# Linear attention: a head's recurrence emitted in eight steps instead of one piece

## The chip, the cores and the metric

The kernel runs on one core of a Trainium2 chip. The core has five engines that the kernel uses: TensorE (PE in the profile; its weight loads are listed apart as PEld), VectorE (DVE), ScalarE (ACT), GpSimd (POOL) and SyncE (SP), whose queue issues the DMA transfers. Each engine works through its own list of instructions in order. The metric is the device time of one execution, in microseconds; the median of the runs is given.

## The reference

The program is one inference step of a network of four layers over 640 tokens (512 latent tokens and 128 context tokens) of 1024 channels. Each layer has another token mixer: HGRN2 (a gated linear recurrence), a gated convolution, an RG-LRU recurrence and latent attention. Each ends in a layer norm. The change touches the first layer, whose mixer is this:

```python
def hgrn2_mixer(h, w_in, lb, norm_g, w_out, s0):
    q, f_fw, f_bw, i, g = jnp.split(h @ w_in, ...)
    q = (jax.nn.silu(q) * HG_KDIM ** -0.5).reshape(b_, n, HG_HEADS, HG_KDIM)
    v = i.reshape(b_, n, HG_HEADS, HG_VDIM)
    for d, fl in enumerate((f_fw, f_bw)):
        f = (lb[d] + (1 - lb[d]) * jax.nn.sigmoid(fl)).reshape(b_, n, HG_HEADS, HG_KDIM)
        args = (q, 1 - f, v, jnp.log(f))        # flipped in time for d == 1
        o, s = gla_chunk(*args, s0[:, d])
    o = rms_norm(outs[0] + outs[1], norm_g.reshape(HG_HEADS, HG_VDIM))
    y = (o.reshape(b_, n, HG_V) * jax.nn.silu(g)) @ w_out
```

There are 8 heads with 128 key and 128 value channels. The function gla_chunk is the recurrence S <- f * S + k v^T, o = q S, taken in chunks: scores inside a chunk (q times decay against k over decay, masked to the causal part), and a state that is carried from chunk to chunk. The states after the last token are outputs too.

## The kernel before, in words

Activations lie with channels on the 128 partitions and the 640 tokens along the row. A product with fp32 accuracy is made of three matmuls on a high part and a low part of both factors. ACT casts the high part of a weight block (wh, L80) and DVE subtracts it from the block for the low part (wl, L82); the cast is marked so that it keeps the place that it has in the program text. `next_w` is called at the start of each product; it returns that product's block and prepares the block that is wanted some products later.

A Python function with a list scheduler behind it writes the program: each operation gets its place in its engine's list in the order of the text, except where the scheduler moves a ready one ahead. In layer 0 (`hgrn`) the loop over `HG_ORDER` goes through the heads ("h") and the gates ("g"). For a head there are two forget products (psmm, 48 matmuls of 128x320: 8 blocks of the inner dimension, three split products, two halves of the tokens), whose tanh is th0 and th1, then the query product (psmm; psmh for head 0) and, for even heads, the value product of two heads (pv: five token tiles of 24 matmuls of 128x256; the first 12 of a tile use one weight block, the other 12 the next). A gate has one product. Small matmuls of the adaLN vectors (psA) are put between.

The function `gla` is the recurrence of one head. Its parts, with the names that the trace shows: f and k from th (ACT, L744, L746); prefix and suffix decays pre and suf as scans (DVE, L748 to L754); inv, the inverse decay, by Ln (ACT, L761, L762) and Exp (ACT, L873), which need two sets of function tables; block decays B, S and kr, ku (DVE); the transposes of ku (pst, PE, L798) and their copy kt (ACT, L800); state updates (psu, PE, L804) and the states s (DVE, L836); scores attS and attP (PE, L849 to L863); outputs po and pp (PE, L885, L887); the RMS norm, with squares on ACT (L893), the mean and the power on POOL (L894, L895) and the scaling on DVE (on, L897); transposes back (pm, pn, PE, L905) and the copies into o (ACT, L906, L907).

Before, `gla(h)` is written in one piece: a hook in `mtile` calls it at the fourth block of the product that follows the head's query and value products. So all casts that the value product wants are already in the text. The last part (pm, pn and the copies) is kept back and written after the second product that follows.

Of the kernel before, what the change touches and what calls it, by code (L numbers as in the profile page):

```python
# [9 lines left out]
F32 = mybir.dt.float32  # L10
F32R = mybir.dt.float32r
U32 = mybir.dt.uint32
AF = mybir.ActivationFunctionType
# [3 lines left out]
P = 128  # L17
D = 1024
KT = D // P
TS_ = 512  # L20
TP = 128
T = TS_ + TP
HALF = T // 2
SPL = (slice(0, 384), slice(384, T))
NT = T // P
# [25 lines left out]
class Kernel:  # L51
# [127 lines left out]
    def mtile(self, nk=KT, xh=None, xl=None, halves=False):  # L179

        nc = self.nc
        xh = self.xh if xh is None else xh
        xl = self.xl if xl is None else xl
        wh, wl = self.next_w()
        if halves:
            ps = [self.psg.tile([P, 512], F32, name="psmh", tag="g") for _ in range(2)]
            out = [p[:, :HALF] for p in ps]
        else:
            ps = self.psmm.tile([P, 2, 512], F32, name="psmm", tag="mm")
            out = ps = ps[:, :, :HALF]  # L190
            ps = [ps[:, hf, :] for hf in range(2)]
        for k in range(nk):
            if self.hook and k == 3:
                hook, self.hook = self.hook, None
                hook()
            for w, x, first, last in ((wh, xh, True, False), (wh, xl, False, False), (wl, xh, False, True)):
                for hf in range(2):
                    nc.tensor.matmul(ps[hf][:, :HALF], lhsT=w[:, k, :], rhs=x[:, k, hf * HALF:(hf + 1) * HALF],  # L198
                                     start=(first and k == 0), stop=(last and k == nk - 1))
        return out  # L200
# [46 lines left out]
    def token_sums(self, pool):  # L247
# [17 lines left out]
        self.split(*t[4], b21)  # L265
        self.tops = t

    def mpair(self):

        nc = self.nc  # L270
        ws = [self.next_w() for _ in range(2)]
        pss = []
        for c in SPL:
            ps = self.psmm.tile([P, 2, 512], F32, name="psmm", tag="mm")
            ps = ps[:, :, :c.stop - c.start]
            for n, (wh, wl) in enumerate(ws):
                hook = None
                if self.pend and n == 1:
                    hook, self.pend = (HOOK, self.pend), None
                self.mm3(ps[:, n, :], [(wh[:, k, :], wl[:, k, :], self.xh[:, k, c], self.xl[:, k, c])  # L280
                                       for k in range(KT)], hook)
            pss.append(ps)
        return pss

# [262 lines left out]
    def start(self):  # L547

        nc, tc = self.nc, self.tc
        with ExitStack() as ctx:  # L550
# [59 lines left out]
            for q in range(4):  # L610
# [4 lines left out]
                        part(q, u)  # L615
                finish(q)

    HG_ORDER = (("h", 0), ("h", 1), ("h", 2), ("g", 0), ("h", 3), ("g", 1), ("h", 4), ("g", 2), ("h", 5), ("g", 3),
                ("h", 6), ("g", 4), ("h", 7), ("g", 5), ("g", 6), ("g", 7))

    def hgrn(self):
        nc, tc, I = self.nc, self.tc, self.I
        with ExitStack() as ctx:
            gc = ctx.enter_context(tc.tile_pool(name="gc", bufs=1))
            g1 = ctx.enter_context(tc.tile_pool(name="g1", bufs=1))
            g2 = ctx.enter_context(tc.tile_pool(name="g2", bufs=2))
# [38 lines left out]
            hng = gc.tile([P, HEADS], F32, name="hng")  # L665
# [1 line left out]
            zb = gc.tile([P, 256], mybir.dt.bfloat16, name="zb")  # L667
            nc.gpsimd.memset(zb, 0.0)
            self.hc = (c0, c1, nc1, hng, m16, mtri, mb, attm, ln64, zb)
            vt, wait = None, 0  # L670
            tails = []
            for kind, h in self.HG_ORDER:
                if (kind, h) == ("g", 6):
                    self.pend = tails.pop()
                    pss = self.mpair()
                    for hf in range(2):
                        for n in range(2):
                            hh = 6 + n
                            sg = self.silu2h(g1, pss[hf][:, n], "silut")
                            oc = self.o[:, hh, SPL[hf]]  # L680
                            nc.vector.tensor_tensor(out=oc, in0=oc, in1=sg, op=ALU.mult)
                    break
                if kind == "g":
                    ps = self.mtile()
                    wait += 1
                    sg = self.silu2h(g1, ps, "silut")
                    nc.vector.tensor_tensor(out=self.hv(self.o[:, h, :]), in0=self.hv(self.o[:, h, :]), in1=sg, op=ALU.mult)
                    continue
                th = []
                for d in range(2):  # L690
                    ps = self.mtile()
                    wait += 1
                    if tails and wait >= 2:
                        tails.pop()()
                    t = g2.tile([P, T], F32, name=f"th{d}", tag=f"th{d}", bufs=1)
                    nc.scalar.activation(out=self.hv(t), in_=ps, func=AF.Tanh, scale=0.5)
                    th.append(t)
                ps = self.mtile(halves=h == 0)
                qt = g1.tile([P, T], F32, name="qt", tag="silut")
                q = g2.tile([P, T], F32, name="q", tag="q")  # L700
                qs = 0.5 * P ** -0.5
                if h == 0:
                    parts = [(self.hv(qt)[:, n], self.hv(q)[:, n], ps[n]) for n in range(2)]
# [7 lines left out]
                if h % 2 == 0:  # L711
                    vt = g2.tile([P, NT, 256], F32, name="vt", tag="vt")
                    ws = [self.next_w() for _ in range(2)]
                    for i0 in range(0, NT, 2):
                        pv = self.psmm.tile([P, 2, 512], F32, name="pv", tag="mm")
                        n = min(2, NT - i0)
                        for i in range(n):
                            tok = slice((i0 + i) * P, (i0 + i + 1) * P)
                            self.mm3(pv[:, i, 0:256], [(self.xh[:, k, tok], self.xl[:, k, tok], ws[k // 4][0][:, k % 4, :],
                                                        ws[k // 4][1][:, k % 4, :]) for k in range(KT)])  # L720
                        nc.scalar.copy(out=vt[:, i0:i0 + n, :], in_=pv[:, 0:n, 0:256])  # L721
                wait = 0
                vh = vt[:, :, (h % 2) * P:(h % 2) * P + P]
                self.hook = lambda h=h, th=th, q=q, vh=vh: tails.append(self.gla(h, th, q, vh, g1, g2, gd))

    def gla(self, h, th, q, vt, g1, g2, gd):
        nc, I = self.nc, self.I
        c0, c1, nc1, hng, m16, mtri, mb, attm, ln64, zb = self.hc
        NB = T // 16

        def b3(ap, a, b):
            return ap.rearrange("p (a b) -> p a b", a=a, b=b)
        qint, states = [], []
        psP = self.psg.tile([P, 2, P], F32, name="attP", tag="g")

        def half(ap, w):
            return ap.rearrange("p (n w b) -> p n w b", w=2, b=16)[:, :, w, :]
# [27 lines left out]
        def direction(d, k, p, r, inv):  # L765
# [17 lines left out]
            if d == 1:  # L783
# [8 lines left out]
            ku = g1.tile([P, T], F32, name="ku", tag="ku")  # L792
            nc.vector.tensor_tensor(out=b3(ku, NB, 16), in0=b3(kr, NB, 16), in1=S[2].unsqueeze(2).to_broadcast([P, NB, 16]),
                                    op=ALU.mult)
            tiles = (0, 1, 2, 4) if d == 0 else (1, 2, 3, 4)
            pst = self.psg.tile([P, 4, P], F32, name="pst", tag="g")
            for n, i in enumerate(tiles):
# [1 line left out]
            kt = g1.tile([P, 4, P], F32, name="kt", tag="kt", bufs=2)  # L799
            nc.scalar.copy(out=kt, in_=pst)  # L800
            yield
            psu = self.psg.tile([P, 4, P], F32, name="psu", tag="g")
            for n, i in enumerate(tiles):
                nc.tensor.matmul(psu[:, n, :], lhsT=kt[:, n, :], rhs=vt[:, i, :], start=True, stop=True)  # L804
            qp = gd.tile([P, T], F32, name="qp", tag="qp")
            nc.vector.tensor_tensor(out=qp, in0=q, in1=p, op=ALU.mult)
            qrel, krel = inv, k
# [9 lines left out]
            for src, scl, n, g, w, nm in ((kr, S[1], 5, 4, er, "kh"), (qp, B[1], 5, 4, la, "qh"),  # L817
# [8 lines left out]
            nc.vector.tensor_tensor(out=b3(qi, 32, 16), in0=b3(qp[:, :TS_], 32, 16),  # L826
                                    in1=B[2][:, :32].unsqueeze(2).to_broadcast([P, 32, 16]), op=ALU.mult)
            qint.append(qi)

            s0 = g2.tile([P, P], F32, name=f"s0{d}", tag=f"s0{d}")  # L830
            nc.sync.dma_start(out=s0, in_=I["state_hgrn"][d, h])
# [8 lines left out]
            fin = g2.tile([P, P], F32, name="fin", tag="fin")  # L840
            nc.scalar.copy(out=fin, in_=psu[:, 3, :])
            nc.sync.dma_start(out=self.O["new_state_hgrn"][d, h], in_=fin)

            psS = self.psg.tile([P, 4, P], F32, name="attS", tag="g")
            pss = [psS[:, i, :] if i < 4 else psP[:, d, :] for i in range(NT)]
            for i, ps in enumerate(pss):
# [24 lines left out]
        inv = [invert(d, *dec[d]) for d in range(2)]  # L871
        for d in range(2):
            nc.scalar.activation(out=inv[d], in_=inv[d], func=AF.Exp, scale=-1.0, bias=ln64[:, 0:1])  # L873
        stages = [direction(d, *dec[d], inv[d]) for d in range(2)]
        for st in stages:
            for _ in st:
                pass
        att = gd.tile([P, T], F32, name="att", tag="suf")
        nc.vector.tensor_tensor(out=att, in0=attm[0], in1=attm[1], op=ALU.add)
        po = self.psg.tile([P, 4, P], F32, name="po", tag="g")  # L880
# [17 lines left out]
                                op=ALU.mult)  # L898
        nc.vector.tensor_scalar(out=on[:, TS_:], in0=pp, scalar1=r5[:, 4:5], scalar2=None, op0=ALU.mult)

        def tail():
            pm = self.psg.tile([P, TS_], F32, name="pm", tag="g")
            pn = self.psg.tile([P, P], F32, name="pn", tag="g")
            for i in range(NT):
                nc.tensor.transpose(pm[:, i * P:(i + 1) * P] if i < 4 else pn, on[:, i * P:(i + 1) * P], self.ident)  # L905
            nc.scalar.activation(out=self.o[:, h, :TS_], in_=pm, func=AF.Copy, scale=hng[:, h:h + 1])  # L906
            nc.scalar.activation(out=self.o[:, h, TS_:], in_=pn, func=AF.Copy, scale=hng[:, h:h + 1])  # L907
        return tail


    def taps(self, y, x, offs, wv):
# [610 lines left out]
    def build(self):  # L1522
# [7 lines left out]
        self.weights(wlist)  # L1530
        self.credit, self.rate = -2.0, 0.0
        self.sw = None
        self.pend = self.hook = None
        self.adaq, self.adafin = [], []
        self.start()
        for l in range(self.NL):
# [158 lines left out]
```

## Time and profile before

| what | value |
|---|---|
| median of 3 runs | 1456.24 us (1455.66 to 1457.84) |
| profiled execution, its time | 1453.07 us |
| its span on the core | 1451.3 us |
| mean granted TensorE clock | 0.995 |
| PE busy | 1401.8 us, 97% of the span |
| DVE busy | 1085.7 us, 75% |
| ACT busy | 751.2 us, 52% |

The span is what the profiler saw from the first to the last instruction. The granted clock is the share of full speed (2.4 GHz) that the throttle gave. Layer 0's products and recurrences lie at about 45 to 440 us of the span.

### The profile page before, as it was taken

The numbers are of one execution on the slowest core, as the hardware profiler recorded it, in microseconds if no ns is written. First come the engines' busy times: TensorE is split into PE (matmuls) and PEld (weight loads), VectorE is DVE, ScalarE is ACT, GpSimd is POOL, SyncE is SP. The second block draws the span as 40 slices with busy tenths as digits, with TensorE's granted clock in tenths as the row PEclk, the third lists the DMA queues.
The fourth block names the chain that finished last, engine by engine and source line by source line (L and its number), as shares of the span: only waits on it lengthen the run. The fifth ranks groups of instructions, "written<-read, shape, count | busy, mean of one in ns | idle before, by whom it ended". The sixth has DMA issues, their size and how long they took to land.

```text
span 1451.3 us, 26592 instructions
## 1 busy us (share of the span) xinstructions
PE 1401.8 (97%) x10762; PEld 1283.0 (88%) x10762; DVE 1085.7 (75%) x1987; ACT 751.2 (52%) x1350; POOL 88.0 (6%) x195
## 2 busy tenths in 40 slices
PE   6999999999999999999999999999999999999997
PEld 4898989989989899999998989899999888888795
DVE  4778587477668778878786999786656868677777
ACT  2657366356543644544426677632642466566630
POOL 0000000000000100000000011100110200000002
PEclk9999999999999999999999999999999999999999
DMA  9322334233246324443452434442213100000041
GB/s 347 121 90 85 100 116 136 82 110 114 85 142 211 139 77 158 146 145 117 143 192 88 146 131 144 139 152 84 67 62 128 57 27 10 25 30 30 30 146 72
DMA packets 51369, 160.50 MB, mean 111 GB/s; under 512 B 5984, under 2 KB 13488, under 8 KB 49456
## 3 DMA queue, kind: packets, MB, share of 16 engines
q1 hardware_dynamic: 51248, 158.82, 32.3%
q8 instruction: 84, 1.38, 0.4%
q14 instruction: 37, 0.30, 0.1%
HBM read 149.69 MB, written 9.10 MB: 109 GB/s over the span
## 4 chain that ended last, share of the span: by engine, by line
PE 70%; DVE 13%; ACT 10%; DMA 4%; issue 3%; POOL 1%; SPq 0%; POOLq 0%; DVEq 0%; ACTq 0%
PE psmm L198 13%; PE psx L217 7%; PE pso L176 4%; PE pso L177 4%; PE pso L175 4%; PE psz L217 3%; PE poa L1447 3%; PE psmm L1078 2%; DVE wl L82 2%; PE ptp L1434 2%; PE psy L217 2%; PE psA L353 2%; DVE tr L1108 1%; PE psmm L176 1%; PE psS L175 1%
## 5 line engine op out<-in xcount | busy, mean ns | idle before, releaser
L198 PE MATMUL psmm<-xh,wh 128*128 128x320 f32 x784 | 183.9, 316 | 2.6 <-ACT vt L721 2.1
L198 PE MATMUL psmm<-xh,wl 128*128 128x320 f32 x784 | 182.8, 312 | 0.0
L198 PE MATMUL psmm<-xl,wh 128*128 128x320 f32 x784 | 180.5, 311 | 0.0
L80 ACT CAST wh<-wraw 128x1024 fp32r<-128x1024 f32 (+4 forms) x129 | 127.2, 998 | 97.9 <-PE pso L177 42.7
L82 DVE TENSOR_TENSOR wl<-wraw,wh 128x1024 fp32r<-128x1024 f32 (+4 forms) x129 | 148.2, 1159 | 27.6 <-ACT wh L80 27.2
L176 PE MATMUL pso<-wl,xh 128*128 128x256 f32 (+1 forms) x464 | 148.7, 321 | 1.5 <-DVE wl L82 1.5
L175 PE MATMUL pso<-wh,xh 128*128 128x256 f32 (+1 forms) x464 | 149.3, 323 | 0.1
L177 PE MATMUL pso<-wh,xl 128*128 128x256 f32 (+1 forms) x464 | 148.5, 320 | 0.0
L198 PEld LDWEIGHTS psmm<-xh,wh 128*128 128x128 f32 x784 | 129.6, 188 | 11.5 <-issue 3.9
L198 PEld LDWEIGHTS psmm<-xh,wl 128*128 128x128 f32 x784 | 131.5, 188 | 1.0 <-issue 0.6
L198 PEld LDWEIGHTS psmm<-xl,wh 128*128 128x128 f32 x784 | 131.1, 188 | 1.4 <-issue 1.2
L176 PEld LDWEIGHTS pso<-wl,xh 128*128 128x128 f32 x464 | 87.4, 188 | 8.7 <-DVE wl L82 2.1
L175 PEld LDWEIGHTS pso<-wh,xh 128*128 128x128 f32 x464 | 87.2, 188 | 7.4 <-ACT xh L163 0.4
L177 PEld LDWEIGHTS pso<-wh,xl 128*128 128x128 f32 x464 | 87.3, 188 | 7.2
L1418 ACT ACTIVATE pe<-psS,mx 128x768 f32<-128x768 f32 (+1 forms) x80 | 63.7, 797 | 38.8 <-DVE mx L1416 38.4
L1416 DVE TENSOR_REDUCE mx<-psS 128x1 f32<-128x768 f32 (+1 forms) x80 | 65.3, 817 | 7.8 <-PE psS L177 7.1
L1434 PE MATMUL ptp<-ident,pe 128*128 128x128 f32 x400 | 56.8, 273 | 0.8 <-ACT pe L1418 0.8
L176 PE MATMUL psmm<-xl,wh 128*128 128x384 f32 (+1 forms) x160 | 49.8, 311 | 0.3 <-DVE xl L166 0.3
L175 PE MATMUL psmm<-xh,wh 128*128 128x384 f32 (+1 forms) x160 | 49.9, 312 | 0.0
L1447 PE MATMUL poa<-pT,v 128*64 128x256 f32 (+1 forms) x416 | 48.8, 377 | 0.7 <-ACT pT L1436 0.4
L177 PE MATMUL psmm<-xh,wl 128*128 128x384 f32 (+1 forms) x160 | 49.2, 308 | 0.0
L1434 PEld LDWEIGHTS ptp<-ident,pe 128*128 128x128 f32 x400 | 46.4, 140 | 2.4 <-ACT pe L1418 1.1
(501 smaller groups left out, 3756.5 us busy)
## 6 DMA issues: line engine op xcount, KB each, us to landing
wraw<-in_wpack SPq DMA_DIRECT2D x109, 512.0 KB
araw<-in_ada_rest SPq DMA_DIRECT2D x80, 512.0 KB
praw<-in_wpack SPq DMA_DIRECT2D x14, 1024.0 KB
araw<-in_ada_first SPq DMA_DIRECT2D x16, 512.0 KB
zdram<-z SPq DMA_DIRECT2D x10, 512.0 KB
gateb<-gate_dram SPq DMA_DIRECT2D x6, 512.0 KB
z<-zdram SPq DMA_DIRECT2D x6, 512.0 KB
wraw<-in_wpack SPq DMA_DIRECT2D x8, 320.0 KB
```

Of the source, the lines that this page charges most:

```text
L80: self.tc.keep_in_program_order(nc.scalar.copy(out=wh[:, :n], in_=raw[:, :n]))
L82: nc.vector.tensor_tensor(out=wl[:, :n], in0=raw[:, :n], in1=wh[:, :n].bitcast(F32), op=ALU.subtract)
L175: nc.tensor.matmul(ps, lhsT=ah, rhs=bh, start=(i == 0), stop=False)
L176: nc.tensor.matmul(ps, lhsT=ah, rhs=bl, start=False, stop=False)
L177: nc.tensor.matmul(ps, lhsT=al, rhs=bh, start=False, stop=(i == n - 1))
L198: nc.tensor.matmul(ps[hf][:, :HALF], lhsT=w[:, k, :], rhs=x[:, k, hf * HALF:(hf + 1) * HALF], start=(first and k == 0), stop=(last and k = ...
L217: nc.tensor.matmul(ps, lhsT=u[:, k, :], rhs=v[:, k, :], start=(first and st and k == 0), stop=(en and k == 3), skip_group_check=True)
L353: nc.tensor.matmul(ps[32 * j:32 * j + 32, :], lhsT=self.csil[:, k, :], rhs=raw[:, j * 256:(j + 1) * 256], start=(k == 2 * u), stop=(k == 2 ...
L1416: nc.vector.reduce_max(out=mx, in_=ps[:, :nk], axis=AX.X, negate=True)
L1418: nc.scalar.activation(out=pe[:, :nk], in_=ps[:, :nk], func=AF.Exp, bias=mx[:, 0:1], accum_out=g["sm"][:, n, hp:hp + 1])
L1434: nc.tensor.transpose(pt[:, kk, :], pe[:, (k0 + kk) * P:(k0 + kk + 1) * P], self.ident)
L1447: nc.tensor.matmul(po[hp * 64:(hp + 1) * 64, 0, :nq], lhsT=v4[:, kt, vc + hp * 64:vc + (hp + 1) * 64], rhs=g["pt"][hp][:, kk, :nq], start= ...
```

## The change

`gla` becomes a generator of eight steps. `hgrn` makes the generator of a head as soon as both th tiles exist, before the query product, and takes the first step at once: decays of both directions, all Ln and Exp, and the block decays, kr and ku of direction 0. The other steps have due times in estimated microseconds; `tick` adds an estimate for each block of a product (0.88), each value tile (2.8) and each half of a pair of gates, and takes every step that is due. The steps go through the two directions in turn (transposes and kt; score operands; psu and states; scores), then come the output and the norm, and last pm and pn with the copies. What is left of a head is taken before the next head's generator begins and, for the last step, after the head's gate product. The order of the heads and gates changes, psu moves behind the score operands, and the tile attP is taken when the first scores are written. The diff, cut:

```diff
...
         for k in range(nk):
-            if self.hook and k == 3:
-                hook, self.hook = self.hook, None
-                hook()
+            self.tick(0.88)
             for w, x, first, last in ((wh, xh, True, False), (wh, xl, False, False), (wl, xh, False, True)):
...
+    def tick(self, us):
...
+        self.now += us
+        for g in list(self.gens):
+            while g in self.gens and g[1] <= self.now:
+                self.step(g)
...
+    def step(self, g):
+        g[3] += 1
+        try:
+            g[1] = g[2] + next(g[0])
+        except StopIteration:
+            self.gens.remove(g)
...
                                        for k in range(KT)], hook)
+                self.tick(24 * (c.stop - c.start) / 2200)
             pss.append(ps)
...
-    HG_ORDER = (("h", 0), ("h", 1), ("h", 2), ("g", 0), ("h", 3), ("g", 1), ("h", 4), ("g", 2), ("h", 5), ("g", 3),
-                ("h", 6), ("g", 4), ("h", 7), ("g", 5), ("g", 6), ("g", 7))
+    HG_ORDER = (("h", 0), ("h", 1), ("g", 0), ("h", 2), ("h", 3), ("g", 1), ("g", 2), ("h", 4), ("h", 5), ("g", 3),
+                ("h", 6), ("h", 7), ("g", 4), ("g", 5), ("g", 6), ("g", 7))
...
             self.hc = (c0, c1, nc1, hng, m16, mtri, mb, attm, ln64, zb)
-            vt, wait = None, 0
-            tails = []
+            vt = None
+            done = {}
...
+            def finish(h, tail=True):
...
+                g = done[h]
+                while g in self.gens and (tail or g[3] < 8):
+                    self.step(g)
             for kind, h in self.HG_ORDER:
                 if (kind, h) == ("g", 6):
-                    self.pend = tails.pop()
                     pss = self.mpair()
+                    finish(7)
                     for hf in range(2):
...
                     ps = self.mtile()
-                    wait += 1
+                    finish(h)
                     sg = self.silu2h(g1, ps, "silut")
...
                     ps = self.mtile()
-                    wait += 1
-                    if tails and wait >= 2:
-                        tails.pop()()
                     t = g2.tile([P, T], F32, name=f"th{d}", tag=f"th{d}", bufs=1)
...
                     th.append(t)
+                if h:
+                    finish(h - 1, False)
+                qv = {}
+                g = [self.gla(h, th, qv, g1, g2, gd), 0.0, self.now, 0]
+                done[h] = g
+                self.gens.append(g)
+                self.step(g)
                 ps = self.mtile(halves=h == 0)
                 qt = g1.tile([P, T], F32, name="qt", tag="silut")
-                q = g2.tile([P, T], F32, name="q", tag="q")
+                q = qv["q"] = g2.tile([P, T], F32, name="q", tag="q")
                 qs = 0.5 * P ** -0.5
...
                                                         ws[k // 4][1][:, k % 4, :]) for k in range(KT)])
+                            self.tick(2.8)
                         nc.scalar.copy(out=vt[:, i0:i0 + n, :], in_=pv[:, 0:n, 0:256])
-                wait = 0
-                vh = vt[:, :, (h % 2) * P:(h % 2) * P + P]
-                self.hook = lambda h=h, th=th, q=q, vh=vh: tails.append(self.gla(h, th, q, vh, g1, g2, gd))
...
-    def gla(self, h, th, q, vt, g1, g2, gd):
+                qv["vt"] = vt[:, :, (h % 2) * P:(h % 2) * P + P]
...
+    def gla(self, h, th, qv, g1, g2, gd):
...
             return ap.rearrange("p (a b) -> p a b", a=a, b=b)
-        qint, states = [], []
-        psP = self.psg.tile([P, 2, P], F32, name="attP", tag="g")
+        qint, states, both = [], [], []
...
+        due = (10, 11, 22.5, 24, 26, 29, 32, 35) if h % 2 == 0 else (8, 9, 12, 15, 18, 21.5, 25, 29)
...
                                     op=ALU.mult)
+            yield
             tiles = (0, 1, 2, 4) if d == 0 else (1, 2, 3, 4)
...
             yield
-            psu = self.psg.tile([P, 4, P], F32, name="psu", tag="g")
-            for n, i in enumerate(tiles):
-                nc.tensor.matmul(psu[:, n, :], lhsT=kt[:, n, :], rhs=vt[:, i, :], start=True, stop=True)
+            q = qv["q"]
             qp = gd.tile([P, T], F32, name="qp", tag="qp")
...
             qint.append(qi)
+            yield
+            vt = qv["vt"]
+            psu = self.psg.tile([P, 4, P], F32, name="psu", tag="g")
+            for n, i in enumerate(tiles):
+                nc.tensor.matmul(psu[:, n, :], lhsT=kt[:, n, :], rhs=vt[:, i, :], start=True, stop=True)
...
+            yield
...
+            if d == 0:
+                both.append(self.psg.tile([P, 2, P], F32, name="attP", tag="g"))
+            psP = both[0]
             psS = self.psg.tile([P, 4, P], F32, name="attS", tag="g")
...
             nc.scalar.activation(out=inv[d], in_=inv[d], func=AF.Exp, scale=-1.0, bias=ln64[:, 0:1])
-        stages = [direction(d, *dec[d], inv[d]) for d in range(2)]
-        for st in stages:
-            for _ in st:
-                pass
+        da, db = [direction(d, *dec[d], inv[d]) for d in range(2)]
...
+        for ds, t in zip(((da,), (da, db), (da,), (da, db), (da, db), (db,), (db,)), due):
+            for st in ds:
+                next(st, None)
+            yield t
+        vt = qv["vt"]
         att = gd.tile([P, T], F32, name="att", tag="suf")
...
-        def tail():
-            pm = self.psg.tile([P, TS_], F32, name="pm", tag="g")
-            pn = self.psg.tile([P, P], F32, name="pn", tag="g")
-            for i in range(NT):
-                nc.tensor.transpose(pm[:, i * P:(i + 1) * P] if i < 4 else pn, on[:, i * P:(i + 1) * P], self.ident)
-            nc.scalar.activation(out=self.o[:, h, :TS_], in_=pm, func=AF.Copy, scale=hng[:, h:h + 1])
-            nc.scalar.activation(out=self.o[:, h, TS_:], in_=pn, func=AF.Copy, scale=hng[:, h:h + 1])
-        return tail
+        yield due[7]
+        pm = self.psg.tile([P, TS_], F32, name="pm", tag="g")
+        pn = self.psg.tile([P, P], F32, name="pn", tag="g")
+        for i in range(NT):
+            nc.tensor.transpose(pm[:, i * P:(i + 1) * P] if i < 4 else pn, on[:, i * P:(i + 1) * P], self.ident)
+        nc.scalar.activation(out=self.o[:, h, :TS_], in_=pm, func=AF.Copy, scale=hng[:, h:h + 1])
+        nc.scalar.activation(out=self.o[:, h, TS_:], in_=pn, func=AF.Copy, scale=hng[:, h:h + 1])
...
         self.sw = None
-        self.pend = self.hook = None
+        self.pend = None
+        self.gens, self.now = [], 0.0
         self.adaq, self.adafin = [], []
```

In the rows that follow, the number behind a name tells tiles of the same name apart. ACT, head 0, from the second forget product's tanh (th1) on. wh4 is the second weight block of the value product, qt the query's tanh. Before:

```order
L696 ACTIVATE th1_575<-psmm_526 128x640
L80 CAST wh4_578<-wraw4_577 128x1024
L744 ACTIVATE f_805<-th0_518,lbc0_461,lbc1_459 128x640
L707 ACTIVATE qt_633<-psmh_583 128x320
L707 ACTIVATE qt_633<-psmh_584 128x320
L80 CAST wh5_642<-wraw5_641 128x1024
```

Changed, from the first Ln of head 0 on (the tanh, f and k stand ahead of it):

```order
L785 ACT_TABLE_LOAD
L785 ACTIVATE inv_599<-suf_585 128x20x16
L786 ACTIVATE inv_599<-pre_583 128x20x16
L785 ACTIVATE inv_602<-pre_594 128x20x16
L905 ACT_TABLE_LOAD
L905 ACTIVATE inv_599<-inv_599,ln64_443 128x640
L786 ACT_TABLE_LOAD
L786 ACTIVATE inv_602<-suf_596 128x20x16
L730 ACT_TABLE_LOAD
L730 ACTIVATE qt_684<-psmh_634 128x320
L905 ACTIVATE inv_602<-inv_602,ln64_443 128x640
L80 CAST wh4_629<-wraw4_628 128x1024
```

The cast of wh4 stood right behind th1 and ahead of the first f; now it stands behind all Ln and Exp of both directions and four table loads.

PE, the value product of head 0, at the passage from its first weight block (wh3, wl3) to its second (wh4, wl4). Before, in the first token tile:

```order
L175 MATMUL pv_653<-wh3_521,xh_102 128x256
L176 MATMUL pv_653<-wl3_522,xh_102 128x256
L177 MATMUL pv_653<-wh3_521,xl_103 128x256
L175 MATMUL pv_653<-wh4_578,xh_102 128x256
L176 MATMUL pv_653<-wl4_579,xh_102 128x256
L177 MATMUL pv_653<-wh4_578,xl_103 128x256
```

Changed (pv_704 is the first token tile pair's first, pv_798 the next bank; the rows begin with the last matmuls that use the first weight block):

```order
L175 MATMUL pv_798<-wh3_521,xh_102 128x256
L176 MATMUL pv_798<-wl3_522,xh_102 128x256
L177 MATMUL pv_798<-wh3_521,xl_103 128x256
L823 MATMUL pst_753<-ident_74,ku_626 128x128 x4
L175 MATMUL pv_704<-wh4_629,xh_102 128x256
L175 MATMUL pv_798<-wh4_629,xh_102 128x256
L176 MATMUL pv_704<-wl4_630,xh_102 128x256
L177 MATMUL pv_704<-wh4_629,xl_103 128x256
```

Before, 12 matmuls with the first block were followed by those with the second. Now 24 with the first block stand ahead, of two banks, then the four transposes, then all that need wh4.

ACT, head 2, from the second forget product on. Before, wh12 is the second weight block of head 2's value product; f, k and inv are head 2's own:

```order
L696 ACTIVATE th1_1601<-psmm_1543 128x640
L906 ACTIVATE o_104<-pm_1592,hng_465 128x512
L907 ACTIVATE o_104<-pn_1593,hng_465 128x128
L80 CAST wh12_1604<-wraw12_1603 128x1024
L744 ACTIVATE f_1875<-th1_1601,lbc0_461,lbc1_459 128x640
L746 ACTIVATE k_1879<-th1_1601,lbc1_459,lbnc1_463 128x640
L762 ACT_TABLE_LOAD
L762 ACTIVATE inv_1886<-pre_1870 128x20x16
L761 ACTIVATE inv_1889<-pre_1881 128x20x16
L873 ACT_TABLE_LOAD
L873 ACTIVATE inv_1886<-inv_1886,ln64_443 128x640
```

Changed, where wh13 is the second weight block of head 2's value product; the rows are head 2's too, and pm_1725 belongs to head 1:

```order
L770 ACTIVATE k_1668<-th1_1651,lbc1_459,lbnc1_463 128x640
L905 ACT_TABLE_LOAD
L905 ACTIVATE inv_1675<-inv_1675,ln64_443 128x640
L785 ACT_TABLE_LOAD
L785 ACTIVATE inv_1678<-pre_1670 128x20x16
L942 ACTIVATE o_104<-pm_1725,hng_465 128x512
L943 ACTIVATE o_104<-pn_1726,hng_465 128x128
L832 COPY k_1668<-kr_1895 128x20x16
L786 ACTIVATE inv_1678<-suf_1672 128x20x16
L905 ACT_TABLE_LOAD
L905 ACTIVATE inv_1678<-inv_1678,ln64_443 128x640
L80 CAST wh13_1719<-wraw13_1718 128x1024
```

Before, wh12 stood right behind th1 and the two copies o, ahead of f and k of the second direction. Now wh13 has k, three table loads, Ln, both Exp and the two copies ahead of it.

Between the last output matmul of a head (pp) and its transposes pm, PE's order of before has 53 or more matmuls of products for the even heads and 17 to 30 for the odd heads; changed, it has 18 for heads 0, 2 and 4, 21 for head 6, and 17 to 24 for the odd heads, with a group of adaLN products beside them at heads 1 and 3. The number of PE instructions is the same.

## Rows read from the trace of the kernel before

**Rows 1.** The page: busy us, share of the span, number of instructions.
```profile
PE 1401.8 (97%) x10762; PEld 1283.0 (88%) x10762; DVE 1085.7 (75%) x1987; ACT 751.2 (52%) x1350; POOL 88.0 (6%) x195
```
**Rows 2.** Stretch: length; busy (instructions) of PE, PEld, DVE, ACT, POOL; clock, DMA share, GB/s.
```profile
45.00:440.00 395.00, 380.60 (x3511) 358.49 (x3510) 285.67 (x588) 224.92 (x377) 16.39 (x56) 1.00 0.33 108
```
**Rows 3.** Waits of PE, 45 to 440 us: us in total, times, longest.
```profile
PE psu L804 <- ACT kt L800: 5.1, 5, 1.5
PE pm L905 <- DVE on L897: 3.1, 4, 1.7
PE attS L849 <- ACT inv L811: 2.4, 2, 1.2
PE psmm L198 <- ACT vt L721: 2.1, 1, 2.1
PE psT L372 <- DVE arows L356: 1.7, 1, 1.7
```
**Rows 4.** ACT in time order, head 0: start, duration, instruction [idle before <-releaser].
```profile
55.68 0.93 ACT L744 ACTIVATE f<-th,lbc,lbc 128x640 f32<-128x640 f32 x1 [1.75 <-DVE lbnc L664]
56.51 0.74 ACT L707 ACTIVATE qt<-psmh 128x320 f32<-128x320 f32 x2
57.15 2.00 ACT L80 CAST wh<-wraw 128x1024 fp32r<-128x1024 f32 x2
...
61.60 1.28 ACT L761 ACT_TABLE_LOAD   x1
62.90 0.47 ACT L761 ACTIVATE inv<-suf 128x320 f32<-128x320 f32 x1
...
66.99 0.83 ACT L873 ACTIVATE inv<-inv,ln 128x640 f32<-128x640 f32 x1
```
**Rows 5.** PE in time order, head 0's value product and the product after it.
```profile
56.11 0.28 PE L175 MATMUL pv<-wh,xh 128*128 128x256 f32 x1
...
72.62 0.56 PE L198 MATMUL psmm<-xh,wh 128*128 128x320 f32 x2 [2.15 <-ACT vt L721]
```
**Rows 6.** DVE in time order, head 0.
```profile
56.71 1.49 DVE L748 TENSOR_TENSOR_SCAN pre<-f,m 128x640 f32<-128x640 f32 x1 [1.04 <-ACT f L744]
...
59.90 2.34 DVE L82 TENSOR_TENSOR wl<-wraw,wh 128x1024 fp32r<-128x1024 f32 x2
...
62.95 0.82 DVE L754 TENSOR_TENSOR pre<-pre,f 128x640 f32<-128x640 f32 x1
```
**Rows 7.** Stretches at the program's start, columns as in rows 2.
```profile
20.00:24.00 4.00, 0.92 (x13) 0.70 (x17) 2.60 (x7) 3.32 (x6) 0.00 (x0) 0.64 1.02 414
24.00:28.00 4.00, 4.00 (x49) 2.49 (x41) 2.30 (x3) 1.02 (x2) 0.00 (x0) 0.51 1.03 420
```
**Rows 8.** ACT, 45 to 440 us, by line: count, busy, mean ns; idle before.
```profile
L696 ACT ACTIVATE th<-psmm 128x640 f32<-128x640 f32 x16 | 11.2, 702 | 23.1 <-PE psmm L198 23.1
L800 ACT COPY kt<-pst 128x512 f32<-128x512 f32 x16 | 9.3, 584 | 20.3 <-PE pst L798 20.3
L906 ACT ACTIVATE o<-pm,hng 128x512 f32<-128x512 f32 x8 | 5.5, 685 | 4.9 <-PE pm L905 4.9
L907 ACT ACTIVATE o<-pn,hng 128x128 f32<-128x128 f32 x8 | 2.9, 364 | 0.0
```
**Rows 9.** All engines in time order, from head 1's outputs to its transposes.
```profile
129.23 0.54 PE L198 MATMUL psmm<-xh,wh 128*128 128x320 f32 x2
...
129.61 0.45 PE L198 MATMUL psmm<-xl,wh 128*128 128x320 f32 x2
...
131.66 0.46 PE L198 MATMUL psmm<-xh,wl 128*128 128x320 f32 x2
...
131.76 1.18 POOL L895 TENSOR_TENSOR r<-r,mhalf 128x5 f32<-128x5 f32 x1
...
132.97 0.69 DVE L897 TENSOR_TENSOR on<-po,r 128x512 f32<-128x512 f32 x1 [5.09 <-POOL r L895]
...
133.81 0.63 PE L905 MATMUL pm<-ident,on 128*128 128x128 f32 x4 [1.69 <-DVE on L897]
```

## The prediction

> **What bounds the kernel now.** I read the page's busy shares first, then the stretches, then TensorE's waits, then the time order of ACT, DVE and PE where the change moves work. The page has PE busy 97% of the span [rows 1]. The change touches layer 0 alone, and from the first output product on PE's order is the same in both programs, so only the stretch from 45 to 440 us counts. There PE is busy 380.6 of 395.0 us at a granted clock of 1.00, ACT 224.9, DVE 285.7 [rows 2]: the stage is bound by PE, and all that a better order can give back is PE's idle 14.4 us. Five waits make it up (5.1 for kt, 3.1 for on, 2.4 for inv, 2.1 for vt, 1.7 for arows) [rows 3]. The number of PE instructions is the same before and after, so the sum is: these waits gone, and the new ones added.
>
> **The change part by part.** I take all 14.4 us as gone, since each of the five places has other neighbours now; where a wait of the same kind comes back, it is counted below as new.
>
> *Head 0's value product.* Casts of weights keep the program's order on ACT. Before, the second value weight's cast (wh4) stood ahead of the recurrence: the two casts at 57.15 to 59.15 run before the first table load at 61.60 [rows 4], and pv ran from 56.11 without a wait up to the one that ends at 72.62 [rows 5]. Now wh4 stands behind both Exp of step 1. ACT starts the first f at about 54.5, not 55.68, because lbnc no longer has one of the low-part subtractions (1.17 each, 2.34 for two) ahead of it [rows 4, 6]. From there to the end of wh4 ACT does two f and two k (3.4, at 0.85 from start to start), 4 table loads of 1.28 (5.1), 4 Ln of 0.47 (1.9), 2 Exp of 0.83 (1.6), one half of qt (0.4) and the cast (1.0): 13.4, and about 0.5 for scans that come late (d = 0's two take 1.49 each and 0.82 follows) [rows 4, 6]. So wh4 is there at 68.4 and its low part at 69.6. PE begins pv at 56.11. Before, 120 products took 72.62 - 2.15 - 56.11 = 14.4, or 0.12 each [rows 5], so the 24 that need only the first weight end at 59.0; four transposes and the few products that need only wh4 give about 0.6. What remains is a wait of about 10.0 us. Its floor is 0, if the cast were as early as before; its ceiling 12, if every scan is waited for.
>
> *The clock at that wait.* None of the stage's waits (2.15 at most) brought the clock below 1.00 [rows 2, 3, 5], but from 20 to 24 us PE was busy 0.92 of 4.00 at 0.64, and in the next 4.00, busy all through, at 0.51 [rows 7]: the 1.2 GHz level. A mean of 0.64 is 2.9 us at half speed, and 4.0 follow, so the low stretch is some 6.8 us; a PE that is busy in all of it loses half, 3.4. A wait of 10 us lies between the two cases; I take 3.4, bounds 0 and 6.8. The Trainium skill says the same kind of thing ("TensorE: Matmul & The Clock Gate", "What's actually happening"): the throttled state is the default and activity releases it. By that rule this wait does cost more than itself, by the rows at 2.15 it would not; the difference is the 3.4.
>
> *Heads 2, 4 and 6.* The same order: the second value weight (wh13 for head 2) now stands behind both Exp; before, wh12 was cast right after th1 and o. From the end of th1's product ACT has th 0.70, table and Ln 1.75, f and k 1.8, a wait of 0.9 for the scan, table and Exp 2.1, table and Ln 1.75, both o copies 1.0, the copy of k 0.46, Ln 0.47, table and Exp 2.1, the cast 1.0: about 14.2 [rows 4, 6, 8]. PE has 48 products of the query at 0.146 ((131.66 - 129.61) / 14) [rows 9], 7.05; eight adaLN products and five transposes back, 1.5; 12 pv, 1.4; four more transposes and the turn between products, 0.6: about 10.55. The wait is 3.65, and with 0.65 of the low part's subtraction 4.3. The same count gives 12.15 against 9.6 at head 4 (2.5) and 19.0 against 13.0 at head 6 (6.0; ACT has an sgh product's table and the previous head's o before it). Together 12.8, bounds 0 and 20.
>
> *The norm.* From pp's last product to the transposes pm lies a chain through ACT (squares), POOL (1.18 for the power) and DVE (on): 4.6 us from 129.23 to 133.81. In head 1 of before 18 products stand between, 2.9, and 1.69 is waited [rows 9]; even heads had 53 or more between and waited nothing, so the 3.1 of [rows 3] was all of odd heads. Now heads 0, 2 and 4 have 18 products between, head 6 has 21: 3 x 1.7 + 1.25. The odd heads have 19 to 24 with adaLN products beside them, or 17: 0, 0.7, 0.95, 1.75. Sum 9.75, bounds 3.1 (the same as now) and 14.
>
> *The state updates.* psu now stands 24 products (3.5) or more behind its transposes, but in odd heads the copy kt comes at the end of step 1's chain on ACT: the terms of the last paragraph but one with the two table loads and qt ahead of kt (0.58) are 13.9 from the end of th1's product, and PE covers about 12.6. That gives 1.35 for heads 1 and 3, and by the same count 2.1 and 1.75 for 5 and 7: 6.55, where it was 5.1 [rows 3, 8]. Bounds 0 and 12. Outputs of head 3 wait 0.45.
>
> *What I cost at nothing.* Eight table loads more in this layer, 10.3 of ACT time [rows 4]: where they stand ahead of a cast or kt they are counted above, elsewhere ACT's 170 idle us hide them [rows 2]. Six more interruptions of a product by small matmuls cost 0.1 each. Loads of weights and states issued up to 10 us later stay off the path: DMA was 0.33 busy in the stretch and no wait of PE was for one [rows 2, 3]. If that cover goes, a 512 KB load is late at the 108 GB/s of this stretch by no more than 5.
>
> **Sum.** -14.4 + 10.0 + 3.4 + 12.8 + 9.75 + 6.55 + 0.45 = +28.5. The profiled execution took 1453.07, so 1481.6 in its terms. The median of the runs is 3.2 above it; with that, 1485.
>
> **The page's rule that speaks most against the change.** After a table load the next instruction starts 0.02 us later here (61.60 + 1.28 to 62.90, and 65.69 to 66.99 the same) [rows 4]. The Trainium skill ("ScalarE: Activation LUTs", "What ACT_TABLE_LOAD costs") adds a drain of about 1380 ns to the load at every switch. By it, as an estimate, four loads before each of the four casts would make those waits 5.5 longer each. The trace disagrees, since the time between the load and its user is 0.02; I give it a case of its own below with a small chance.
>
> **The rivals.**
> *1. Only head 0 and the norm wait.* ACT runs ahead at heads 2, 4 and 6 and kt arrives in time. For it: their margins are differences of two sums, 2.5 at head 4, and ACT is busy only 57% [rows 2]. Against: the instructions stand in one queue and the order shows the cast behind two table loads and Exp. -14.4 + 10.0 + 3.4 + 9.75 = +8.75: 1465.
> *2. Not slower: the casts are in time everywhere.* The mechanism: the idle 14.4 is given back since every small matmul comes later than its operands, and step 1, begun ahead of the query product, ends on ACT before the value product's 25th matmul. It decides at head 0: ACT would have to do 13.4 in the 4.5 from 54.5 to 59.0. With the norm's waits left, -14.4 + 9.75 = -4.65: 1451.6. With the norm as it is now (3.1), 1445. For it: DVE and ACT have idle time, and psu, attS and po stand further behind what they need. Against: the first table load to the end of the first Exp alone takes 61.60 to 67.8 now, more than the 4.5 [rows 4].
> *3. The clock falls at the long waits of heads 2, 4 and 6 too.* +3.4 each: 1495. Against: waits of 2.15 did not do it [rows 5].
> *4. Table loads cost more than their rows show:* four waits of 5.5 more at most, 1507; no gap behind a load speaks for it [rows 4].
>
> **How the numbers follow.** Forecast, the four casts late: 0.71, with its own range 1470 to 1497 (head 6's term is the least sure, and the clock's). Rival 1: 0.14. Rival 2: 0.08, of which 0.05 ends more than 0.2% (3 us, about what a measurement of this kernel can tell from no change) below 1456.2, and 0.03 within it. Rival 3: 0.05. Rival 4: 0.02. The range that leaves out 2 in 10 takes in rival 1's middle and rival 3's: 1462 to 1498. Slower by more than 0.2%: 0.92.
>
> **What the changed profile would show.** PE in the value product of head 0 waits for wh4 or its low part, some 10 us from 59, and the slice behind it has a granted clock near 0.5 for a few us; the same wait at heads 2, 4, 6 of 4.3, 2.5, 6.0; a wait of pm for on in every even head near 1.7; kt waits of 1 to 2 in odd heads; none for vt and arows. PE's idle time in the stage is then about 39, not 14. I am wrong if head 0's value product waits under 5, or if the casts at heads 2 to 6 end before PE asks for them: then the gain side (14.4) decides, and the time falls to rival 1 or 2.

## The result, and the profile after

The changed kernel takes 1481.11 us (1479.99 to 1482.34, 4 runs) against 1455.95 (1453.48 to 1457.84, 4 runs) before: a ratio of 1.0175, 95% interval 1.0163 to 1.0187. It is 25 us slower; the forecast was slower, at 1485.

The profiled execution's span is 1478.2 us, 26.9 longer than before. First the page's line of busy times, and of the page's groups the value products' first matmuls (count, busy us, mean ns of one, idle before it).

```profile
PE 1409.3 (95%) x10762; PEld 1289.4 (87%) x10762; DVE 1089.1 (74%) x1987; ACT 762.0 (52%) x1358; POOL 87.0 (6%) x195
...
L175 PE MATMUL pv<-wh,xh 128*128 128x256 f32 x160 | 48.9, 308 | 7.9 <-ACT wh L80 7.4
```

The number of PE instructions is that of [rows 1], but PE is busy 7.5 us longer and still holds a smaller share. PE's waits in layer 0, now 45 to 470 us, answer to [rows 3]:

```profile
PE pm L941 <- DVE on L933: 9.3, 7, 1.7
PE pv L175 <- ACT wh L80: 7.4, 3, 3.1
PE pst L823 <- DVE ku L817: 6.3, 1, 6.3
PE psu L856 <- ACT kt L825: 5.3, 4, 1.7
PE psT L385 <- DVE arows L369: 3.8, 2, 2.4
PE pv L176 <- DVE wl L82: 1.4, 3, 0.5
PE pv L175 <- DVE mods L391: 0.5, 1, 0.5
PE po L921 <- DVE att L915: 0.2, 1, 0.2
```

They sum to 34.2 us, 14.4 before: 19.8 more. The other 7.1 of the 26.9 is PE working slower, as its busy time says too (1409.3 against 1401.8). PE in time order at head 0's value product, beside [rows 5]:

```profile
58.18 0.28 PE L177 MATMUL pv<-wh,xl 128*128 128x256 f32 x1
64.73 1.11 PE L823 MATMUL pst<-ident,ku 128*128 128x128 f32 x4 [6.27 <-DVE ku L817]
67.90 0.80 PE L175 MATMUL pv<-wh,xh 128*128 128x256 f32 x2 [2.06 <-ACT wh L80]
69.16 0.58 PE L176 MATMUL pv<-wl,xh 128*128 128x256 f32 x1 [0.46 <-DVE wl L82]
...
71.04 0.41 PE L175 MATMUL pv<-wh,xh 128*128 128x256 f32 x1
71.25 0.41 PE L176 MATMUL pv<-wl,xh 128*128 128x256 f32 x1
...
72.65 0.28 PE L176 MATMUL pv<-wl,xh 128*128 128x256 f32 x1
72.77 0.28 PE L177 MATMUL pv<-wh,xl 128*128 128x256 f32 x1
```

One stall is told in three waits: the transposes stand ahead of wh4's matmuls and wait for ku, then the cast is late, then its low part: 8.8. Until 72 a value matmul starts every 0.21 (the 1.2 GHz level), then every 0.12. ACT in time order shows why the cast is late (beside [rows 4]):

```profile
54.01 0.92 ACT L768 ACTIVATE f<-th,lbc,lbc 128x640 f32<-128x640 f32 x1 [1.67 <-DVE lbnc L677]
...
57.40 1.28 ACT L785 ACT_TABLE_LOAD   x1
58.69 0.47 ACT L785 ACTIVATE inv<-suf 128x320 f32<-128x320 f32 x1
...
66.10 0.82 ACT L905 ACTIVATE inv<-inv,ln 128x640 f32<-128x640 f32 x1
66.82 1.03 ACT L80 CAST wh<-wraw 128x1024 fp32r<-128x1024 f32 x1
```

The cast stands behind the last Exp and ends at 67.85 (66.82 + 1.03); PE was done with the first weight block at 58.46 (64.73 - 6.27). The stretches (columns as in rows 2; the clock is the third figure from the end) show the half clock, for all or part of a stretch, at four places, the value products of heads 0, 2, 4 and 6:

```profile
64.00:68.00 4.00, 1.21 (x5) 0.81 (x5) 3.94 (x13) 3.97 (x6) 0.00 (x0) 0.50 0.01 4
68.00:72.00 4.00, 3.54 (x15) 3.24 (x16) 3.96 (x5) 3.27 (x6) 0.00 (x0) 0.50 0.40 132
72.00:76.00 4.00, 4.00 (x36) 4.00 (x36) 4.00 (x10) 0.94 (x2) 0.00 (x0) 1.00 0.70 261
164.00:168.00 4.00, 4.00 (x24) 2.96 (x24) 3.53 (x6) 1.19 (x2) 0.00 (x0) 0.57 0.42 131
268.00:272.00 4.00, 4.00 (x28) 4.00 (x28) 3.93 (x7) 1.59 (x3) 0.00 (x0) 0.76 0.40 131
372.00:376.00 4.00, 4.00 (x22) 4.00 (x21) 3.86 (x12) 0.46 (x1) 0.00 (x0) 0.53 0.92 296
```

The stalls ahead of the last three, and the norm's wait at head 0, whose row answers to the last of [rows 9]:

```profile
106.79 0.63 PE L941 MATMUL pm<-ident,on 128*128 128x128 f32 x4 [1.56 <-DVE on L933]
...
162.50 0.39 PE L175 MATMUL pv<-wh,xh 128*128 128x256 f32 x1 [3.12 <-ACT wh L80]
...
266.67 0.66 PE L385 MATMUL psT<-ident,arows 128*128 128x128 f32 x2 [2.38 <-DVE arows L369]
...
369.13 0.80 PE L175 MATMUL pv<-wh,xh 128*128 128x256 f32 x2 [2.18 <-ACT wh L80]
```

Head 4's is not the cast: the transposes of the adaLN rows (arows) wait for DVE, and by then the cast is done. It comes from the same chain by another way: on DVE arows stands behind a product with inv, which began at 265.69 after 1.14 of waiting for step 1's last Exp (264.83 to 265.66 on ACT).

### The profile page after: what moved, and what is told of

Same layout as the page of the kernel before. It is cut to its first block, busy times and chain, and to the rows that moved or that the text cites. A ratio compares the mean times of both kernels' runs of the same rounds, so it can differ in the third digit from the quotient of the medians.

```text
span 1478.2 us, 26627 instructions
## 1 busy us (share of the span) xinstructions
PE 1409.3 (95%) x10762; PEld 1289.4 (87%) x10762; DVE 1089.1 (74%) x1987; ACT 762.0 (52%) x1358; POOL 87.0 (6%) x195
## 4 chain that ended last, share of the span: by engine, by line
PE 72%; ACT 12%; DVE 10%; issue 2%; DMA 2%; POOL 1%; SPq 0%; POOLq 0%; DVEq 0%; ACTq 0%
PE psmm L196 13%; PE psx L215 7%; PE pso L176 4%; PE pso L177 4%; PE pso L175 4%; PE psz L215 3%; PE poa L1482 3%; PE psmm L1113 2%; PE ptp L1469 2%; PE psA L366 2%; PE psy L215 2%; PE psmm L176 1%; DVE tr L1143 1%; DVE wl L82 1%; PE psmm L177 1%
## 5 line engine op out<-in xcount | busy, mean ns | idle before, releaser
L175 PE MATMUL pv<-wh,xh 128*128 128x256 f32 x160 | 48.9, 308 | 7.9 <-ACT wh L80 7.4
```

The lines of the kernel that those rows point to most:

```text
L175: nc.tensor.matmul(ps, lhsT=ah, rhs=bh, start=(i == 0), stop=False)
```

## The experiments

Each was timed beside the kernel before on the same chip; where a time is set beside the changed kernel's, that is 1481.11. The kernel before took 1454.2 to 1457.5 in these rounds (their medians), so such a difference can be off by some 2 us.

**cast_early.** The second value weight is cast ahead of step 1:

```diff
                 self.gens.append(g)
+                if h % 2 == 0:
+                    self._prep()
                 self.step(g)
```

> The changed kernel, with one cast moved: for even heads the second weight block of the value product is prepared ahead of step 1, so that it stands on ACT ahead of f, k, Ln and Exp. Theory (the casts behind both Exp are the largest loss): PE's waits for wh and wl in the value products (8.8 us) go, and with them the low clock behind them at heads 2 and 6 (some 4). Head 0's transposes wait for ku less, about 3 instead of 6.3, since 59 value matmuls stand ahead of them and no longer 24. Some 15 to 19 less than the changed kernel: 1462 to 1466. Rival (ACT and DVE are simply late with step 1, whatever stands in front of the cast): the waits turn up again at ku, kt and qt, at most 5 less: 1476 or more.

1463.44 us, 1.0045 of before (1.0029 to 1.0061), 17.7 less than the changed kernel: the time that the theory had. PE's waits (the longest four rows), and the stretches at heads 0 and 6:

```profile
PE pm L943 <- DVE on L935: 9.4, 7, 1.7
PE psu L858 <- ACT kt L827: 5.3, 4, 1.7
PE pst L825 <- DVE ku L819: 3.2, 1, 3.2
PE psT L385 <- DVE arows L369: 2.8, 1, 2.8
```

```profile
64.00:68.00 4.00, 2.44 (x12) 2.45 (x13) 4.00 (x18) 3.96 (x7) 0.03 (x1) 0.61 0.00 0
352.00:356.00 4.00, 4.00 (x24) 4.00 (x24) 2.35 (x13) 3.99 (x6) 0.00 (x0) 0.62 0.07 28
```

No wait for wh or wl is left, ku is waited for 3.2, and pm and kt are as they were. The span fell by 18.1 (to 1460.1) and the waits by 10.3 (to 23.9): 7.8 is left over. Part of it is the slow stretches: they are gone at heads 2 and 4, but not at head 0 (behind the wait for ku) and not at head 6, where the theory had them end and the wait for arows stands ahead of one. Added up over stretches of 1 us, what PE's busy time lost at a lower clock is 8.7 in the changed kernel and 3.1 here. So the casts cost both, some 10 of waits and some 5.6 of clock; the other 2 or so are not traced.

**cast_early_h0.** The same edit for head 0 alone (`if h == 0`).

> The changed kernel, with the second value weight's cast ahead of step 1 for head 0 alone. Theory (each head's stall is its own): head 0's 8.8 of waits become some 3.2, and of its low clock, about 2.2, half goes; heads 2 to 6 stay. 6 to 8 less than the changed kernel: 1473 to 1475. Rival (a late head 0 pushes the later heads, so that the first stall feeds those behind it): as cast_early for all heads, 1463 to 1468.

1473.78, 1.0114 of before (1.0098 to 1.0129), 7.3 less than the changed kernel. The waits at heads 2 and 6 are as in the changed kernel (3.12 and 2.19 for wh). Each head's stall is its own; head 0 is some 40% of what cast_early gains.

**step1_early.** The kernel before, with step 1's decays, Ln and Exp written ahead of the query product, and nothing else of the change:

```diff
+                qv = {}
+                gen = self.gla(h, th, qv, g1, g2, gd)
+                next(gen)
                 ps = self.mtile(halves=h == 0)
...
+        yield
+        q, vt = qv["q"], qv["vt"]
...
         stages = [direction(d, *dec[d], inv[d]) for d in range(2)]
```

> The kernel before, with one part of the change: the decays, Ln and Exp of a head are written ahead of its query product, the rest of the recurrence in one piece where it was; order of heads and norm as before. Theory: this alone puts wh4 behind both Exp, so head 0 loses 9 to 10 and about 2 by the clock, heads 2, 4 and 6 together 4 to 10, and up to 5 of the old waits for inv and vt go: 1464 to 1474. Rival (the spreading of the steps, the norm and the order of heads cost the time, not the early step): 1453 to 1459.

1477.63, 1.0139 of before (1.0124 to 1.0154): the early step alone makes the kernel 20 us slower, more than the 8 to 18 expected. The waits that are new or longer:

```profile
PE pst L800 <- DVE ku L795: 6.6, 1, 6.6
PE pm L910 <- DVE on L902: 6.2, 4, 1.9
...
PE pv L175 <- DVE q L713: 4.8, 2, 3.9
PE pv L175 <- ACT wh L80: 3.4, 2, 1.7
```

Head 0's stall is as in the changed kernel (6.58 + 1.75 + 0.72 = 9.05, against 8.8). What I had missed is q: the query's tanh stands behind the same Ln and Exp on ACT, and the value products of heads 2 and 6 wait for the bank that it frees. The wait for on has doubled too (3.1 before), and the waits for inv, which were to go, stayed (3.2).

**order_alone.** The kernel before with the new order of heads and gates.

> The kernel before, with the changed order of heads and gates alone. Theory: no cast moves behind an Exp, so within 4 us of before, 1452 to 1460. Rival (a gate fewer between two heads gives the recurrence less cover, so the order costs the time): 1465 or more.

1456.0 (10 runs), 0.9989 of before (0.998 to 0.9999): no more than 0.2% either way. The order by itself is not the cause.

**norm_later.** The last step due later, and on taken from qp's buffers so that it may live that long:

```diff
-        due = (10, 11, 22.5, 24, 26, 29, 32, 35) if h % 2 == 0 else (8, 9, 12, 15, 18, 21.5, 25, 29)
+        due = (10, 11, 22.5, 24, 26, 29, 32, 40) if h % 2 == 0 else (8, 9, 12, 15, 18, 21.5, 25, 33)
...
-        on = gd.tile([P, T], F32, name="on", tag="pre")
+        on = gd.tile([P, T], F32, name="on", tag="qp")
```

> The changed kernel, with the last step (pm, pn and the copies) due later, 40 for even heads and 33 for odd ones, and the tile on taken from the buffers of qp so that it may live longer: 49 or more products then lie between a head's outputs and pm, not 17 to 24. Theory: PE's waits of pm for on (9.3 us) go, nothing else does: 1470 to 1474. Rival (the wait only moves on, since ACT is late with what follows): 1478 to 1482.

1463.99, 1.0047 of before (1.003 to 1.0064): 17.1 less than the changed kernel, where 9.3 was expected. The norm's wait is gone, and so is more:

```profile
PE pst L823 <- DVE ku L817: 6.3, 1, 6.3
PE pv L175 <- ACT wh L80: 4.2, 3, 2.1
...
PE psu L856 <- ACT kt L825: 1.5, 2, 0.8
```

The kt waits fell from 5.3 to 1.5, those for wh from 7.4 to 4.2, and the program has 41 table loads instead of 59 (ACT is busy 738.4 us, not 762.0). The tile on had held one of the two buffers of pre until pm, and the next head's decays came later for it.

**on_own_place.** To part the two edits: the buffer alone, the due times as changed.

> The changed kernel, with the tile on taken from the buffers of qp and not from those of pre; due times as changed. It tells apart the two parts of norm_later's gain of 17. Theory: on held one of the two pre buffers until pm, so the next head's decays came late and ACT's Ln and Exp fell into more groups (59 table loads in the changed kernel, 41 in norm_later); that part alone gives the kt waits (3.8) and some of the casts' waits (2 to 3) back, and the norm's own wait stays where 17 to 22 products lie between outputs and pm, at three or four heads (5 to 6 of the 9.3). 8 to 12 less than the changed kernel: 1469 to 1473. Rival (the distance alone gave the 17): 1479 to 1483.

1475.52, 1.0146 of before (1.0123 to 1.0169): 5.6 less than the changed kernel, where 8 to 12 was expected. The 41 table loads are there and no wait for kt is left, so the buffer does what the theory says. But the norm's wait grew:

```profile
PE pm L941 <- DVE on L933: 15.1, 7, 2.7
PE pst L823 <- DVE ku L817: 6.3, 1, 6.3
PE psT L385 <- DVE arows L369: 2.4, 1, 2.4
```

PE, no longer held at kt, comes to pm earlier against the same chain. The longer waits also cost clock, at four heads; the first of them:

```profile
202.70 0.63 PE L941 MATMUL pm<-ident,on 128*128 128x128 f32 x4 [2.69 <-DVE on L933]
...
204.00:208.00 4.00, 4.00 (x20) 4.00 (x20) 2.11 (x2) 3.94 (x7) 0.00 (x0) 0.65 0.00 0
```

Of norm_later's 17.1, the buffer gives 5.6 (4.2 by the two ratios to the kernel before, 1.0146 and 1.0175), and the distance, with the buffer there, the other 11.5, more than the 9.3 it was sized at, since it also takes away what the buffer's gain had turned into.

**both_mended.** cast_early and norm_later together, head 7's last step left at 29, and head 0's transposes due at 16 (`due = (16, 17) + due[2:]`).

> The changed kernel with three edits together: the cast of the second value weight ahead of step 1 (as cast_early), the last step later with on in qp's buffers (as norm_later; head 7 keeps its due time 29), and head 0's transposes due at 16 and not 10. Theory: what remains of PE's waits is some 4 us for the adaLN transposes (arows), 1 to 2 for kt, 1 to 2 for others, 7 to 8 in all where before has 14.4, and little low clock. Some 6 less than before: 1449 to 1453. Rival (the gains of cast_early and norm_later, 18 and 17, are partly the same time, since norm_later also shortens ACT's chain ahead of the casts, and new waits for ku and q come up): 1454 to 1460.

1446.01 (5 runs), 0.9922 of before (0.991 to 0.9935): 11 us faster than the kernel before, where some 6 was expected, and 35 faster than the changed one. That is about the sum of the two gains (17.7 and 17.1), but the third edit is in it too (no wait for ku is left, 3.2 in cast_early, and no low clock at head 0), and it was not run alone. So the 35 does not show that the two gains do not overlap. The waits and the stretches at head 0:

```profile
PE pv L175 <- ACT vt L747: 3.3, 1, 3.3
PE psu L860 <- ACT kt L829: 1.7, 2, 0.9
PE pm L945 <- DVE on L937: 1.6, 1, 1.6
PE psT L385 <- DVE arows L369: 1.2, 1, 1.2
```

```profile
68.00:72.00 4.00, 0.73 (x6) 0.56 (x5) 3.81 (x8) 4.00 (x8) 0.00 (x0) 1.00 0.00 0
72.00:76.00 4.00, 4.00 (x35) 4.00 (x34) 4.00 (x8) 2.57 (x6) 0.00 (x0) 1.00 0.73 246
```

The waits come to some 9.4 (the longest four rows are shown), 5.0 less than before, with the clock at 1.00. Its span is 8.7 shorter than before's (1442.6); of the other 3.7, 2.8 is PE busy for less (1399.0 against 1401.8). Which matmuls that is was not tried, so where these 3.7 come from is open.

## Why the prediction was right

The direction and the size held, and by the step that was named: the cast of the second value weight behind both Exp. cast_early shows it from one side (the waits for wh and wl end), step1_early from the other (they come with that part of the change alone). The norm's place and its buffer cost about as much (17.1 in norm_later); the forecast had the norm's wait in its sum, the buffer not. By terms, in us:

| term | predicted | measured in the changed kernel |
|---|---|---|
| head 0's value product | 10.0 | 8.8 (6.27 + 2.06 + 0.46) |
| heads 2, 4, 6 | 4.3 + 2.5 + 6.0 | 3.6 + 2.4 + 4.6 |
| norm | 9.75 | 9.3 |
| kt | 6.55 | 5.3 |
| po | 0.45 | 0.2 |
| old waits gone | -14.4 | -14.4 |
| clock | 3.4 | 7.1 (what is left of 26.9; 8.7 by stretches of 1 us) |
| sum | 28.5 | 26.9 |

- *Head 0.* ACT's time was right to half a microsecond: the cast ends at 67.85, forecast 68.4, since lbnc came at 54.0 and not 54.5. I had the transposes as cover; they were themselves late, and the wait shows first at ku.
- *Heads 2 to 6.* Head 2's was the cast (3.12 + 0.44). At head 4 the mechanism was wrong and the size right by chance: no wait for wh23, but 2.38 for arows, a wait that I had counted as gone. At head 6 the cast is 2.18 + 0.46, the rest again arows and mods (1.40 + 0.52). DVE's queue, in which arows stands behind step 1's scans and what waits for its Exp, was missing from my working; in cast_early the wait for arows stays at head 6 (2.8). Two slips stand in the sum as well: head 2's terms on ACT add up to 14.0 and not 14.2, and the low part's 0.65 was put in at head 2 alone.
- *Norm and kt* were sized well, but as distances alone. Behind both stood a cause that I did not see in the diff: on and pre share buffers, and an earlier step 1 meets a later pm. on_own_place shows it for kt, whose waits end with the buffer alone; the norm's wait grows there, so its 9.3 came out right while PE was held up at kt.
- *The clock* was the term mis-sized: 3.4 for one place, 7.1 at four; at head 0 itself the stretches above give only some 2.4 (half of 1.21 + 3.54), since PE was idle for much of the slow time. I took the 2.15 wait of [rows 5] as proof that short waits keep the clock. In the changed kernel it fell behind 3.12 + 0.44, 2.38 and 2.18 + 0.46. So part of the third rival came true, and two errors, waits too long by 5.3 and clock too small by 3.7, mostly cancelled.
- *Rivals.* The first (only head 0 and the norm wait) fails on the waits at heads 2 and 6; the second on head 0's 8.8. Table loads cost what their rows show: 57.40 + 1.28 to the Ln at 58.69. By the Trainium skill ("ScalarE: Activation LUTs", "What ACT_TABLE_LOAD costs"), which adds a drain of about 1380 ns to each load, the cast would, as an estimate for the four loads ahead of it, have come some 5.5 later than it did; this trace disagrees. The number of loads is not the loss either: step1_early has 43, fewer than the 51 of before, and is 20 us slower.

## What to carry to other kernels

Where an engine's list holds both a long chain that can wait and a short operation that the bottleneck engine wants soon (a weight cast), look at which stands first after the change: one call that puts the cast ahead was worth 18 us here. A step that begins earlier meets whatever still holds its buffers; read the tile tags beside the due times. And mend before judging: the same steps with the cast, the buffer and some due times put right are 0.8% faster than the kernel before.

## What the runs showed of the hardware

The length of one wait does not tell whether TensorE's clock falls: PE waited 3.27 us in both_mended and 2.15 in the kernel before [rows 5] at a granted clock of 1.00, yet 2.38 at head 4 of the changed kernel was followed by value matmuls at 0.21 us each, the 1.2 GHz level, where 0.12 is normal. Nor did 2.18 for on lower it in on_own_place, where 2.67 to 2.74 did at four heads. These runs do not settle what decides it. The price in the changed kernel is 7 to 9 us over four such places, about as much as its waits for wh and wl (7.4 + 1.4).
